# The scan of an RWKV-7 layer: products in 64x64 quarters of TensorE, keys scaled by a diagonal product, and another order within a chunk

## The chip, the cores and the metric

The kernel runs on one core of a Trainium2 chip. Its metric is the device time of one execution in microseconds (us). Several runs give a median; one more execution was recorded by the hardware profiler, and its span and its rows are what the text reads. Engines are named as in the profile: PE (TensorE's matrix products), PEld (its weight loads), DVE (VectorE), ACT (ScalarE), POOL (GpSimd), SP (SyncE, which here issues most DMAs). "L1700" is line 1700 of the kernel's file. PSUM is the memory that PE writes, in banks of 512 float32 columns.

## What is computed

A two-layer decoder trunk on 1024 positions of width 1024, in float32: an RG-LRU block, cross-attention into 256 memory tokens and an MLP in layer 0; RWKV-7 time mixing, cross-attention and an MLP in layer 1. The change lies in the RWKV-7 mixer, whose recurrence per head (16 heads of 64) is, cut from the reference:

```python
def step(state, inp):
    r_t, w_t, k_t, v_t, a_t, b_t = inp
    sa = jnp.einsum('bhij,bhj->bhi', state, a_t)
    state = (state * w_t[:, :, None, :] + sa[..., None] * b_t[:, :, None, :]
             + v_t[..., None] * k_t[:, :, None, :])
    y_t = jnp.einsum('bhij,bhj->bhi', state, r_t)
    return state, y_t
```

Then y is normalised per head, scaled, shifted, given a bonus term and a gate, and multiplied by w_o.

## The kernel before, in words

Projections, decays, Gram matrices and triangular inverses of all positions are made ahead, and parked in DRAM: a and r rows (MVd), b and k rows (STd), inverses (XTd), values (Vd), gates (G1d, G2d). The scan then walks through 16 chunks of 64 positions. Eight feature tiles q of 128 partitions hold two heads each: head half h is the partition half `hr[h]`. A chunk's heads are worked on in two groups, m (or g) = 0 and 1, of four tiles each.

For each chunk c a tile `sv` holds, per head, the state in the partition half `hr[h]` and the chunk's values in the other. The steps, with their lines in the kernel before:

- `scan_scale` (L1689, POOL): multiplies b and k by the decay at the chunk's end (`pcc`). Two instructions of 128x512.
- `scan_gram` (L1700, PE): products of b and k with a and r, 128 x 128 per head, in two PSUM banks, one for each h. `scan_mask` (L1710, DVE): times a triangular mask, into `gw`. L1712 (ACT): a itself is copied over one corner of `gw`, after the mask.
- `scan_keys` (L1724, PE; L1725, ACT): transposes the scaled b and k into `gk`.
- `values` (L1811, PE; L1813, ACT): W = `gw` times `sv`, copied out of PSUM. It needs the state, and both mask and corner of `gw`.
- `decayed` (L1818, POOL): the state times the decay, into `pcs`.
- `from_state` (L1823, PE): r times the state, the first part of the output Y.
- `solved` (L1829, PE; L1831, DVE): the inverse times W, scaled by `db` (1/d), written over the state's half of `sv`.
- `update` (L1836, PE; L1838, DVE): `gk` times `sv`, plus `pcs`: the state of chunk c + 1.
- `output` (L1843, PE; L1845, ACT): the rest of Y, and its copy out.
- `post_var` (L1736, ACT: eight squarings with sums; L1738 and L1739, POOL), `post_norm` (L1744, DVE), `flip_out` (L1751, PE transposes; L1756, DVE; L1757, POOL): normalisation, turning and gating of chunks c - 1 and c - 2.

Gram, mask and keys are those of chunk c + 1, made a chunk ahead. The order within a chunk is a list, `todo`, written out by hand; a wrapper pins what it calls to that order on each engine. So each engine works its steps off as a queue: an instruction that waits holds all behind it. Other work (the splitting of w_o into two parts, L233 and L234) is put between by a scheduler, which also orders SP's queue, except where it is pinned.

Loads are made for two chunks at a time: L1645 (b and k), L1648 (a and r, four buffers that are filled far ahead), L1659 (inverses), L1672 (values), L1676 (gates). They come from a pool of 45 buffers "u"; a load is issued when a buffer is free. Two PSUM pools of four banks serve the scan. Most matmul loops run over h inside q, so neighbouring products use different halves of PE's rows or columns; the tile position follows from the operands' partitions. One earlier step, the Gram matrices of the preparation (L1418), already gives 64x64 tile positions in all four quarters in turn:

```python
for par, h in ((0, 0), (1, 1), (1, 0), (0, 1)):
    sc = slice((2 * c + par) * 64, (2 * c + par) * 64 + 64)
    mm(pg[h][hr[par], c * 64:c * 64 + 64], a[hr[h], sc], at[hr[h], sc], start=True, stop=True, tile_position=(h * 64, par * 64))
```

Of the kernel before, what the change touches and what calls it, by code (L numbers as in the profile page):

```python
# [1281 lines left out]
def rwkv(self, X, xt, lw_wa, lw_g, post, mid):  # L1282
# [214 lines left out]
        xts[f] = XT  # L1497

    def merge_store(f):
        MQ(nc, f).dma_start(XTd[:, f, :], xts.pop(f))  # L1500

    def aside(step):

# [67 lines left out]
    def evac_v(f, p):  # L1571
        cs = slice(f * 128, f * 128 + 128)
        vt = self.unit()
        nc.scalar.copy(vt, p)
        if f == 1:

            self.depth, self.ahead = DA
            with self.behind():
                self.advance(self.taken - 1)
        pr, kp = ld.pop(f)  # L1580
        nc.vector.scalar_tensor_tensor(pr, pr, self.col("r_k", f), kp, ALU.mult, ALU.mult)
        prs = self.split(pr)


        if f % 2 == 0:
            vk[:] = [self.unit() for _ in range(2)]
        for e in range(2):
            pt = self.bank()
            for i in range(4):
                tt = e * 4 + i  # L1590
                mm(pt[:, i * 128:i * 128 + 128], vt[:, tt * 128:tt * 128 + 128], self.center, start=True, stop=True)
            nc.scalar.copy(vk[e].rearrange("p (t h g i) -> p t h g i", h=2, g=2, i=64)[:, :, :, f % 2, :],
                           pt.rearrange("p (t h i) -> p t h i", h=2, i=64))
            if f % 2 and e == 0:

                for d in range(2):
                    for h in range(2):
                        nc.sync.dma_start(sv0[d][hr[1 - h], h * 512 + (f - 1) * 64:h * 512 + (f + 1) * 64],
                                          vk[0].rearrange("p (t h i) -> p t h i", h=2, i=128)[hr[d], 0, h, :])
            if f % 2:  # L1600
                for h in range(2):
                    nc.sync.dma_start(Vd[e * 512:e * 512 + 512, h, (f - 1) * 64:(f + 1) * 64].rearrange("(t p) i -> p t i", p=128),
                                      vk[e].rearrange("p (t h i) -> p t h i", h=2, i=128)[:, :, h, :])
        g1 = self.unit()
        for e in range(2):
            s = slice(e * 512, e * 512 + 512)
            bp = self.bank()
            for i in range(2):
                mm(bp, self.ones_r, prs[i][:, s], start=i == 0, stop=i == 1)
            nc.vector.tensor_mul(vt[:, s], vt[:, s], bp)  # L1610
            gp = self.bank()
            self.mm3(gp, (g2[0][:, cs], g2[1][:, cs]), (hg[0][:, s], hg[1][:, s]), True, True)
            nc.scalar.activation(g1[:, s], gp, AF.Copy, scale=self.col("gn_g", f))
            nc.vector.scalar_tensor_tensor(vt[:, s], vt[:, s], self.col("gn_b", f), gp, ALU.add, ALU.mult)
        for src, dst in ((g1, G1d), (vt, G2d)):
            for h in range(2):
                nc.sync.dma_start(dst[(f % 2) * 64:(f % 2) * 64 + 64, (f // 2) * 2 + h, :], src[h * 64:h * 64 + 64, :])

    def early(f):
        cs = slice(f * 128, f * 128 + 128)  # L1620
# [10 lines left out]
    def load(n):  # L1631
# [7 lines left out]
        mv = mvb[n % 4]  # L1639
        sts = []  # L1640
        for g in range(2):
            st = self.unit().rearrange("p (e q w t) -> p e q w t", e=2, q=4, w=2)
            for e in range(2):
                es = slice(n * 128 + e * 64, n * 128 + e * 64 + 64)
                nc.sync.dma_start(st[:, e], STd[:, 4 * g:4 * g + 4, :, es])  # L1645
            sts.append(st)
        for w in range(2):
            nc.sync.dma_start(mv[:, :, w, :], MVd[:, :, w, ts])  # L1648
        pcs = self.unit().rearrange("p (e q t) -> p e q t", e=2, q=8)
        for e in range(2):  # L1650
            c, cs = 2 * n + e, slice(e * 64, e * 64 + 64)
            cst[c] = dict(st=[t[:, e] for t in sts], mv=mv[:, :, :, cs],
                          pcs=pcs[:, e], pcc=self.pc[:, c * 8:c * 8 + 8].unsqueeze(2), gw=[])

    def load_solved(n):
# [7 lines left out]
    def load_late(n):  # L1663
# [13 lines left out]
        for e in range(2):  # L1677
            cst[2 * n + e].update(sv=svs[e], gs=gs)

    def scan_scale(c):  # L1680

        if c >= 15:
            return
        s = cst[c]
        s["sc"] = self.unit()
        scv = s["sc"].rearrange("p (q w t) -> p q w t", q=8, w=2)
        for g in range(2):
            qs = slice(4 * g, 4 * g + 4)
            nc.gpsimd.tensor_tensor(scv[:, qs], s["st"][g], s["pcc"][:, qs].unsqueeze(3).broadcast_to([128, 4, 2, 64]), ALU.mult)  # L1689

    def scan_gram(c, g):

# [2 lines left out]
        s = cst[c]  # L1695
        s["pv", g] = [self.bank(h).rearrange("p (q w) -> p q w", q=4) for h in range(2)]
        for q in range(4):
            for h in range(2):
                with self.line("gram"):
                    mm(s["pv", g][h][:, q, :], s["st"][g][hr[h], q].rearrange("p w t -> p (w t)"), s["mv"][hr[h], 4 * g + q],  # L1700
                       start=True, stop=True)

    def scan_mask(c, g):
        if c >= 16:
# [7 lines left out]
            nc.scalar.copy(gw[hr[h], :, h, 0:64], s["mv"][hr[h], 4 * g:4 * g + 4, 0, :])  # L1712
        s["gw"].append(gw)

    def scan_keys(c, g):

        if c >= 15:
            return
        s = cst[c]
        if not g:  # L1720
            s["gk"] = self.unit().rearrange("p (q h i) -> p q h i", q=8, h=2)
        tp = self.bank(g).rearrange("p (q h i) -> p q h i", q=4, h=2)
        for q in range(4):
            nc.tensor.transpose(tp[:, q].rearrange("p h i -> p (h i)"), s["sc"][:, (4 * g + q) * 128:(4 * g + q) * 128 + 128], self.ident)  # L1724
        nc.scalar.copy(s["gk"][:, 4 * g:4 * g + 4], tp)  # L1725
# [52 lines left out]
    for c in range(2):  # L1778
        scan_scale(c)
        for g in range(2):  # L1780
            scan_gram(c, g)
            scan_mask(c, g)
            scan_keys(c, g)
    load_late(0)
    self.psum_layout("banks")
    for h in range(2):
        nc.gpsimd.memset(cst[0]["sv"][hr[h], :, h, :], 0.0)
    for c in range(16):
        if c == 15:
            self.psum_layout("mixed")  # L1790
# [4 lines left out]
                    load_solved(c // 2 + 1)  # L1795
                load_late(c // 2 + 1)
        s = cst[c]
        sv, mv, pcc, xtc, pcs = s["sv"], s["mv"], s["pcc"], s["xt"], s["pcs"]
        dbv = self.db[:, 0:128].rearrange("p (q a t) -> p q a t", a=2, t=8)[:, :, c % 2, c // 2:c // 2 + 1]
        W, U, S, wsb = [], [], [], []  # L1800
        y = self.unit()
        yp = self.bank(c)
        Y = yp.rearrange("p (q i) -> p q i", i=64)

        def values(m):

# [1 line left out]
            reg = [ph[:, x * 256:x * 256 + 256].rearrange("p (q i) -> p q i", i=64) for x in range(2)]  # L1808
            W.append(reg[0]); U.append(reg[1]); S.append(reg[0])
            for q, h in heads:  # L1810
                mm(W[m][hr[h], q, :], s["gw"][m][:, q, h, 0:64], sv[:, m * 4 + q, h, :], start=True, stop=True)  # L1811
            w_ = y[:, 512 + m * 256:768 + m * 256].rearrange("p (q i) -> p q i", i=64)
            nc.scalar.copy(w_, W[m])  # L1813
            wsb.append(w_)

        def decayed(m):
            for h in range(2):
                nc.gpsimd.tensor_tensor(pcs[hr[h], m * 4:m * 4 + 4, :], sv[hr[h], m * 4:m * 4 + 4, h, :],  # L1818
                                        pcc[hr[h], m * 4:m * 4 + 4].broadcast_to([64, 4, 64]), ALU.mult)

        def from_state(m):
            for q, h in heads:
                mm(Y[hr[h], m * 4 + q, :], mv[hr[h], m * 4 + q, 1, :], sv[hr[h], m * 4 + q, h, :],  # L1823
                   start=(m == 0 and q == 0), stop=False)

        def solved(m):
            qs = slice(m * 4, m * 4 + 4)
            for q, h in heads:
                mm(U[m][hr[h], q, :], xtc[hr[h], m * 4 + q, :], wsb[m][hr[h], q, :], start=True, stop=True)  # L1829
            for h in range(2):  # L1830
                nc.vector.tensor_tensor(sv[hr[h], qs, h, :], U[m][hr[h]], dbv[hr[h], qs].broadcast_to([64, 4, 64]), ALU.mult)  # L1831

        def update(m):
            qs = slice(m * 4, m * 4 + 4)
# [5 lines left out]
        def output():  # L1840
            for m in range(2):
                for q, h in heads:
                    mm(Y[hr[h], m * 4 + q, :], s["gw"][m][:, q, h, 64:128], sv[:, m * 4 + q, h, :], start=False,  # L1843
                       stop=(m == 1 and q == 3))
            nc.scalar.copy(y[:, 0:512], yp)  # L1845
# [34 lines left out]
    w = I["b_w_o"][0]  # L1880
    rows = []
    for q in range(4):
        for h in range(2):
# [51 lines left out]
```

## Time and profile before

| | us |
|---|---|
| median of 3 runs | 2841.48 |
| lowest and highest | 2838.39, 2846.89 |
| profiled execution | 2839.18 |
| its span | 2837.5 |
| PE busy, whole span | 2765.8 (97%) |
| DVE, ACT, POOL busy | 1867.1, 1422.8, 907.3 |
| scan, first values burst to last output | about 1741 to 1893 |

The profiled execution took 1.7 us more than its span, which runs from its first to its last recorded instruction. A timeline row gives a start in us from the span's start, the time covered, the engine, the line, the operation, output and input names, partitions x elements, and how many instructions were merged; in brackets, what the engine waited for. For matmuls "64*128" are the rows and columns of the array in use. A float32 product is two PE instructions, a transpose one. "Granted clock" is the share of TensorE's full clock that the throttle let through. A row of a group of instructions ends with busy time, mean duration in ns, and the idle time ahead of them.

### The profile page before, as it was taken

What the parts mean: (1) busy time and instruction counts of PE and PEld (TensorE: products, weight loads), DVE (VectorE), ACT (ScalarE), POOL (GpSimd) and SP (SyncE); (2) the same over time, 40 slices, a digit from 0 to 9 for tenths busy, and PEclk for the clock granted to TensorE, in tenths of its full rate; (3) what the DMA queues carried; (4) which work ended last, traced back from release to release, by engine and by line L of the source; (5) the groups of instructions that cost most, each with busy time, mean ns of one, the idle gap of its engine ahead of it and who ended that gap; (6) DMA issues with size and microseconds to landing.
All of it is one profiled execution on the core that took longest, in us unless ns stands there. A gap on an engine that the chain in (4) does not pass through costs nothing.

```text
span 2837.5 us, 42691 instructions
## 1 busy us (share of the span) xinstructions
PE 2765.8 (97%) x16955; PEld 2310.6 (81%) x16955; DVE 1867.1 (66%) x2017; ACT 1422.8 (50%) x2194; POOL 907.3 (32%) x962
## 2 busy tenths in 40 slices
PE   7999999999999999999999999999999999999998
PEld 6888788888888888887777777888888888888887
DVE  5477557658454577898685834785675755467778
ACT  6456355545545553346672534664563644555333
POOL 2000113014666510013088223853203376640002
PEclk9999999999999999999999999999999999999999
DMA  8212352323454554423558799962222355474453
GB/s 266 75 45 75 104 171 79 103 84 104 148 164 153 206 205 156 155 98 126 170 146 228 218 247 244 238 158 96 79 93 89 99 167 162 141 244 168 149 177 120
DMA packets 383912, 421.92 MB, mean 149 GB/s; under 512 B 91504, under 2 KB 294496, under 8 KB 383712
## 3 DMA queue, kind: packets, MB, share of 16 engines
q1 hardware_dynamic: 371680, 379.19, 44.1%
q0 software_dynamic: 11568, 39.41, 3.8%
q8 instruction: 133, 2.18, 0.3%
q14 instruction: 67, 0.55, 0.1%
q10 hardware_dynamic: 464, 0.59, 0.1%
HBM read 283.79 MB, written 134.74 MB: 148 GB/s over the span
## 4 chain that ended last, share of the span: by engine, by line
PE 44%; DVE 4%; ACT 2%; DMA 2%; issue 1%; SPq 1%; POOL 1%; DVEq 0%; POOLq 0%; ACTq 0%
PE q L318 8%; PE q L319 8%; PE q L320 8%; PE p L318 4%; PE p L320 4%; PE p L319 4%; PE q L1700 1%; DVE u L234 1%; DMA u<-d 1%; PE q L1811 1%; PE q L1823 1%; PE q L1348 1%; PE q L1724 1%; DMA u<-in_b_w_rkv 1%; PE q L1836 0%
## 5 line engine op out<-in xcount | busy, mean ns | idle before, releaser
L234 DVE TENSOR_TENSOR u<-u,u 128x1024 fp32r<-128x1024 f32 (+1 forms) x602 | 813.0, 1381 | 346.4 <-ACT u L233 331.1
L233 ACT CAST u<-u 128x1024 fp32r<-128x1024 f32 (+1 forms) x602 | 591.8, 1020 | 446.6 <-DVE u L1077 224.6
L318 PE MATMUL q<-u,u 128*128 128x512 f32 (+1 forms) x1952 | 744.7, 383 | 4.4 <-DVE u L370 2.1
L319 PE MATMUL q<-u,u 128*128 128x512 f32 (+1 forms) x1952 | 745.0, 382 | 0.0
L320 PE MATMUL q<-u,u 128*128 128x512 f32 (+1 forms) x1952 | 739.7, 382 | 0.0
L318 PE MATMUL p<-u,u 128*128 128x512 f32 (+1 forms) x1472 | 553.5, 378 | 14.5 <-ACT u L233 6.4
L319 PE MATMUL p<-u,u 128*128 128x512 f32 (+1 forms) x1472 | 552.5, 375 | 3.7 <-DVE u L234 3.5
L320 PE MATMUL p<-u,u 128*128 128x512 f32 (+1 forms) x1472 | 551.2, 375 | 4.0 <-DVE u L234 3.9
L328 POOL TENSOR_SCALAR s<-s 128x1 f32<-128x1 f32 x97 | 43.7, 451 | 1252.0 <-ACT u L326 1250.1
L318 PEld LDWEIGHTS q<-u,u 128*128 128x128 f32 x1952 | 366.9, 188 | 77.3 <-ACT u L361 1.5
L320 PEld LDWEIGHTS q<-u,u 128*128 128x128 f32 x1952 | 366.8, 188 | 71.2
L319 PEld LDWEIGHTS q<-u,u 128*128 128x128 f32 x1952 | 367.0, 188 | 70.1
L318 PEld LDWEIGHTS p<-u,u 128*128 128x128 f32 x1472 | 279.7, 190 | 67.1 <-issue 8.6
L320 PEld LDWEIGHTS p<-u,u 128*128 128x128 f32 x1472 | 279.9, 190 | 55.2 <-DVE u L234 6.2
L319 PEld LDWEIGHTS p<-u,u 128*128 128x128 f32 x1472 | 280.1, 190 | 54.4 <-DVE u L234 6.7
L443 POOL TENSOR_TENSOR u<-u,u 128x512 f32<-128x512 f32 x120 | 188.1, 1573 | 6.2 <-PE q L319 2.6
L1135 DVE TENSOR_TENSOR z<-z,q 128x512 f32<-128x512 f32 x192 | 130.7, 683 | 80.2 <-PE q L320 80.2
L320 PE MATMUL q<-z,u 128*128 128x512 f32 x320 | 124.5, 389 | 2.1 <-DVE u L234 2.1
L318 PE MATMUL q<-z,u 128*128 128x512 f32 x320 | 124.8, 390 | 0.0
L319 PE MATMUL q<-z,u 128*128 128x512 f32 x320 | 124.5, 389 | 0.0
L444 POOL TENSOR_TENSOR u<-u 128x512 f32<-128x512 f32 x40 | 68.2, 1704 | 146.2 <-DVE u L234 102.9
L1032 POOL TENSOR_TENSOR u<-u,u 128x512 f32<-128x512 f32 x32 | 46.1, 1441 | 181.7 <-ACT u L1021 172.6
(253 smaller groups left out, 3321.5 us busy)
## 6 DMA issues: line engine op xcount, KB each, us to landing
u<-d SPq DMA_DIRECT2D x194, 512.0 KB, 4.8
d<-u SPq DMA_DIRECT2D x109, 512.0 KB, 3.0
d<-u POOLq DMA_DIRECT2D x68, 512.0 KB, 3.7
d<-u SPq DMA_DIRECT2D x132, 256.0 KB, 3.4
u<-in_m_w_up SPq DMA_DIRECT2D x64, 512.0 KB, 5.4
u<-in_m_w_down SPq DMA_DIRECT2D x64, 512.0 KB, 7.3
u<-in_c_w_kv SPq DMA_DIRECT2D x32, 512.0 KB, 6.5
u<-in_b_w_rkv SPq DMA_DIRECT2D x24, 512.0 KB, 7.1
```

The costliest lines, as they stand in the source:

```text
L233: self.nc.scalar.copy(hv, src)
L234: (eng or self.nc.vector).tensor_tensor(lv, src, hv, ALU.subtract)
L318: mm(o, ah, bh, start=first, stop=False, **kw)
L319: mm(o, ah, bl, start=False, stop=False, **kw)
L320: mm(o, al, bh, start=False, stop=last, **kw)
L328: nc.gpsimd.tensor_scalar(v, ss, 1.0 / n, eps, ALU.mult, ALU.add)
L443: sub = lambda o, x, y: nc.gpsimd.tensor_tensor(o, x, y, ALU.subtract)
L444: nc.gpsimd.tensor_tensor(s[:, a], f1[:, a], f1[:, b], ALU.add)
L1032: tt(s1, r21, r22, ALU.add)
L1135: nc.vector.tensor_add(to_, to_, o)
L1348: mm(p, wa2[i][r, cs], hwa[j][r, s], start=n == 0, stop=n == 2)
L1700: mm(s["pv", g][h][:, q, :], s["st"][g][hr[h], q].rearrange("p w t -> p (w t)"), s["mv"][hr[h], 4 * g + q], start=True, stop=True)
```

## The change

It touches the scan, and what is stored for it.

- `scan_gram` makes four 64x64 products per head pair instead of two of 64x128. `scan_keys` no longer transposes: b and k in quarters are multiplied by a diagonal matrix of the decays, which `scan_scale` makes from an identity `id64` in one POOL instruction of 128x512. The keys' PSUM is split by h instead of by group.
- `values`, `from_state`, `output` and `solved` write W, U and Y of head half h and group m to the partition half h xor m. So `from_state` and `solved` can run over the four pairs of `quads`, each in another quarter. Y gets two banks, one for each m, and two copies. The inverses and gates of tiles 4 to 7, and the rows of w_o, are stored or loaded with their halves swapped to fit.
- b and k are loaded with both chunks of a pair in one DMA: runs of 128 elements instead of 64, four DMAs of 256 KB become two of 512 KB. The inverses are stored in two DMAs of 64 partitions instead of one of 128.
- `decayed` of chunk c + 1 and `scan_scale` of c + 2 follow the update of chunk c.
- `todo` has another order.

```diff
     def scan_gram(c, g):
...
-            for h in range(2):
+            for h, w in quads:
                 with self.line("gram"):
-                    mm(s["pv", g][h][:, q, :], s["st"][g][hr[h], q].rearrange("p w t -> p (w t)"), s["mv"][hr[h], 4 * g + q],
-                       start=True, stop=True)
+                    mm(s["pv", g][h][hr[w], q, :], s["st"][g][hr[h], q, w, :], s["mv"][hr[h], 4 * g + q],
+                       start=True, stop=True, tile_position=(h * 64, w * 64))
...
+    quads = [(0, 0), (1, 1), (0, 1), (1, 0)]
...
-        for g in range(2):
-            qs = slice(4 * g, 4 * g + 4)
-            nc.gpsimd.tensor_tensor(scv[:, qs], s["st"][g], s["pcc"][:, qs].unsqueeze(3).broadcast_to([128, 4, 2, 64]), ALU.mult)
+        s["sc"] = self.unit()[:, 0:512].rearrange("p (q i) -> p q i", i=64)
+        nc.gpsimd.tensor_tensor(s["sc"], self.id64.unsqueeze(1).broadcast_to([128, 8, 64]),
+                                s["pcc"].broadcast_to([128, 8, 64]), ALU.mult)
...
+        for q in range(8):
+            for h, w in quads:
+                mm(tps[h][hr[w], q, :], s["st"][q // 4][hr[h], q % 4, w, :], s["sc"][hr[h], q, :],
+                   start=True, stop=True, tile_position=(h * 64, w * 64))
+        for h in range(2):
+            nc.scalar.copy(s["gk"][:, :, h, :], tps[h])
...
+        def from_state():
+            Y.extend(self.bank(m)[:, 0:256].rearrange("p (q i) -> p q i", i=64) for m in range(2))
+            for q in range(4):
+                for h, m in quads:
+                    mm(Y[m][hr[h ^ m], q, :], mv[hr[h], m * 4 + q, 1, :], sv[hr[h], m * 4 + q, h, :],
+                       start=q == 0, stop=False, tile_position=(h * 64, (h ^ m) * 64))
+
+        def solved():
+            for q in range(4):
+                for h, m in quads:
+                    r = h ^ m
+                    mm(U[m][hr[h], q, :], xtc[hr[r], m * 4 + q, :], wsb[m][hr[r], q, :], start=True, stop=True,
+                       tile_position=(r * 64, h * 64))
...
-        todo = [(decayed, 0), (decayed, 1)] if c < 15 else []
-        if c:
-            todo += [(scan_scale, c + 1)]
-        todo += [(values, 0), (from_state, 0), (values, 1), (from_state, 1)]
+        more = c and c < 15
+        todo = [(values, 0), (values, 1), (from_state,)]
         if c:
             todo += [(post_var, c - 1)]
-        todo += [(solved, 0), (solved, 1)]
+        if more:
+            todo += [(scan_gram, c + 1, 0), (scan_mask, c + 1, 0)]
+        todo += [(solved,)]
+        if more:
+            todo += [(scan_keys, c + 1), (scan_gram, c + 1, 1)]
+        if c < 15:
+            todo += [(update, 0), (update, 1), (decayed, c + 1), (scan_scale, c + 2)]
+        todo += [(output,)]
+        if more:
+            todo += [(scan_mask, c + 1, 1)]
         if c > 1:
             todo += [(flip_out, c - 2)]
-        if c:
-            todo += [(scan_gram, c + 1, 0)]
-        if c < 15:
-            todo += [(update, 0), (update, 1)]
-        if c:
-            todo += [(scan_keys, c + 1, 0), (scan_keys, c + 1, 1), (scan_mask, c + 1, 0), (scan_gram, c + 1, 1), (scan_mask, c + 1, 1)]
-        todo += [(output,)]
         if c:
             todo += [(post_norm, c - 1)]
```

How the instructions then stand: on DVE, one chunk late in the scan, before. L1831 multiplies by 1/d, L1756 gates a turned chunk, L1838 adds the state, L1710 masks, L1744 normalises; "q" is a PSUM bank, "u" a buffer.

```order
L1831 TENSOR_TENSOR u_16112<-q_16646,db 64x256 x2
L1831 TENSOR_TENSOR u_16112<-q_16664,db 64x256 x2
L1756 TENSOR_TENSOR u_16553<-q_16713,u_15762 128x8x64
L1838 TENSOR_TENSOR u_16462<-u_16106,q_16646 64x256 x2
L1838 TENSOR_TENSOR u_16462<-u_16106,q_16664 64x256 x2
L1710 TENSOR_TENSOR u_16763<-q_16720,mask 128x4x128
L1710 TENSOR_TENSOR u_16763<-q_16721,mask 128x4x128
L1710 TENSOR_TENSOR u_16778<-q_16768,mask 128x4x128
L1710 TENSOR_TENSOR u_16778<-q_16769,mask 128x4x128
L1744 TENSOR_TENSOR u_16472<-u_16472,g_16682 128x512
```

And now, a chunk at the same place; L1843 is the multiplication, L1850 the addition, L1768 the gating, L1756 the normalisation.

```order
L1756 TENSOR_TENSOR u_16568<-u_16568,g_16813 128x512
L1710 TENSOR_TENSOR u_17069<-q_17051,mask 128x4x128
L1710 TENSOR_TENSOR u_17069<-q_17052,mask 128x4x128
L1843 TENSOR_TENSOR u_16558<-q_17012,db 64x256
L1843 TENSOR_TENSOR u_16558<-q_17002,db 64x256 x2
L1843 TENSOR_TENSOR u_16558<-q_17012,db 64x256
L1850 TENSOR_TENSOR u_16561<-u_16555,q_17002 64x256 x2
L1850 TENSOR_TENSOR u_16561<-u_16555,q_17012 64x256 x2
L1710 TENSOR_TENSOR u_17193<-q_17131,mask 128x4x128
L1710 TENSOR_TENSOR u_17193<-q_17132,mask 128x4x128
L1768 TENSOR_TENSOR u_17203<-q_17198,u_16131 128x8x64
```

The first two masks moved from behind the additions to ahead of the multiplications; the last two stay behind the additions.

On SP, ahead of chunk 2, before: "z" are the buffers of a and r, L1676 loads gates, L1672 values.

```order
L1648 DMA z_14688<-d_10180 128x8x128 x4
L1676 DMA u_14412<-d_10177 128x8x128
L1676 DMA u_14413<-d_10178 128x8x128
L1672 DMA u_14422<-d_10175 64x512 x2
L1672 DMA u_14425<-d_10175 64x512 x2
```

And now:

```order
L1648 DMA z_14819<-d_10180 128x8x128 x4
L1648 DMA z_13731<-d_10180 128x8x128
L1676 DMA u_14494<-d_10177 128x8x128
L1676 DMA u_14495<-d_10178 128x8x128
L1672 DMA u_14508<-d_10175 64x512 x2
L1672 DMA u_14511<-d_10175 64x512 x2
```

A fifth load of a and r, for a later pair of chunks, moved ahead of the values of chunks 2 and 3.

More of the change, by code (lines that the diff above doesn't have):

```diff
@@ L1641, in load @@
         for g in range(2):
[L1642 to L1645, printed above, removed]
+            st = self.unit().rearrange("p (q w t) -> p q w t", q=4, w=2)
+            nc.sync.dma_start(st, STd[:, 4 * g:4 * g + 4, :, ts])
             sts.append(st)
@@ L1651, in load @@
             c, cs = 2 * n + e, slice(e * 64, e * 64 + 64)
[L1652 removed]
+            cst[c] = dict(st=[t[:, :, :, cs] for t in sts], mv=mv[:, :, :, cs],
                           pcs=pcs[:, e], pcc=self.pc[:, c * 8:c * 8 + 8].unsqueeze(2), gw=[])
@@ L1787, in rwkv @@
         nc.gpsimd.memset(cst[0]["sv"][hr[h], :, h, :], 0.0)
+    decayed(0)
     for c in range(16):
@@ L1814, in values @@
             wsb.append(w_)
[L1816 to L1831, printed above, removed]
+        def from_state():
[10 more added lines that the diff above has]
+                       tile_position=(r * 64, h * 64))
+            for m in range(2):
+                qs = slice(m * 4, m * 4 + 4)
+                for h in range(2):
+                    nc.vector.tensor_tensor(sv[hr[h], qs, h, :], U[m][hr[h]], dbv[hr[h], qs].broadcast_to([64, 4, 64]), ALU.mult)
         def update(m):
@@ L1882, in rwkv @@
     for q in range(4):
-        for h in range(2):
+        for h in (0, 1) if q < 2 else (1, 0):
             rows.append([w[(2 * q + pp) * 128 + h * 64:(2 * q + pp) * 128 + h * 64 + 64, :] for pp in range(2)])
```

42 lines of the change are left out of this document (22 added, 20 removed).

## The prediction

> **What bounds the kernel now.** I read the busy time by stretches first, then the timeline of one chunk engine by engine, then the waits and SP's queue. The change touches only the scan of the RWKV-7 layer, some 150 of 2837.5 us. Busy time in it (us, PE, PEld, DVE, ACT, POOL, granted clock, DMA share, GB/s):
>
> ```profile
> 1740.00:1760.00 20.00, 16.33 (x383) 14.44 (x381) 11.73 (x23) 9.02 (x33) 11.24 (x14) 1.00 0.95 259
> 1760.00:1770.00 10.00, 10.00 (x189) 8.94 (x186) 5.38 (x12) 4.25 (x22) 4.74 (x6) 0.83 1.12 253
> 1770.00:1870.00 100.00, 99.21 (x2150) 88.77 (x2146) 74.71 (x144) 62.18 (x263) 81.95 (x94) 1.00 1.04 239
> ```
>
> From 1770 on PE is full. One chunk on PE (start, time covered, line, shape, instructions; a float32 product is two instructions):
>
> ```profile
> 1798.27 1.15 PE L1843 MATMUL q<-u,u 128*64 128x64 f32 x32
> ...
> 1800.43 0.69 PE L1811 MATMUL q<-u,u 128*64 128x64 f32 x16
> 1801.05 0.68 PE L1823 MATMUL q<-u,z 64*64 64x64 f32 x16
> 1801.56 1.10 PE L1829 MATMUL q<-u,u 64*64 64x64 f32 x32
> 1802.60 0.66 PE L1751 MATMUL q<-ident,u 128*128 128x128 f32 x4
> 1803.18 1.16 PE L1700 MATMUL q<-z,u 64*128 64x128 f32 x16
> 1804.27 1.15 PE L1836 MATMUL q<-u,u 128*64 128x64 f32 x32
> 1805.35 1.09 PE L1724 MATMUL q<-ident,u 128*128 128x128 f32 x8
> 1806.38 1.16 PE L1700 MATMUL q<-z,u 64*128 64x128 f32 x16
> 1807.47 0.74 PE L1843 MATMUL q<-u,u 128*64 128x64 f32 x18
> ```
>
> From output to output this chunk takes 9.20 us with no pause. An instruction of 64 columns lasts 218 ns (group row below), so 32 of them in 1.10 us follow one another every (1.10 - 0.22)/31 = 28.5 ns; 16 are 0.455 us. Yet values (L1811) to from_state (L1823) is 0.62: where the tile shape changes, 0.16 us go by. Nine such places cost 1.4 us a chunk. The average chunk, between the second values bursts of chunks 2 and 14, takes (1877.78 - 1761.36)/12 = 9.70 us:
>
> ```profile
> 1759.36 1.02 PE L1811 MATMUL q<-u,u 128*64 128x64 f32 x16 [2.79 <-DMA u<-d]
> 1760.31 1.12 PE L1823 MATMUL q<-u,z 64*64 64x64 f32 x16
> 1761.36 1.12 PE L1811 MATMUL q<-u,u 128*64 128x64 f32 x16
> ...
> 1877.78 0.93 PE L1811 MATMUL q<-u,u 128*64 128x64 f32 x16
> ...
> 1892.89 0.50 PE L318 MATMUL p<-u,u 128*128 128x512 f32 x1
> ```
>
> **The change on PE.** Its form of product runs already, in the Gram matrices of the preparation (L1418: 64x64, all four quarters in turn):
>
> ```profile
> 1376.42 1.16 PE L1418 MATMUL q<-u,u 64*64 64x64 f32 x64
> 1377.51 0.73 PE L1348 MATMUL q<-u,u 64*128 64x512 f32 x4
> ```
>
> That is (1.16 - 0.22)/63 = 15.0 ns each, half of 28.5. So per chunk: from_state and solved, 32 instructions each, fall from 0.91 to 0.48 (estimate 32 x 15.0). The keys become 64 of them, 0.96, against eight transposes that also start 1.09 before what follows. The two Gram bursts had both row halves at work on 128 columns in 1.09 - 0.16 = 0.93 each; cut into quarters they are twice as many instructions, each half as wide, and I leave 0.93. Values, update, output and flip stay: 0.91, 0.91, 0.91, 0.47. Work: 0.48 + 0.48 + 0.96 + 1.86 + 2.73 + 0.47 = 6.98. The shape now changes four times (values to from_state, Gram to update, output to flip, flip to values): 0.64. PE falls to 7.6 us a chunk. If PE still set the pace, that were 2.1 x 12 = 25 us.
>
> **The change in the order.** I think PE no longer sets it. The groups of the stretch 1770 to 1866, ten chunks (busy, mean ns), and starts on DVE and ACT:
>
> ```profile
> L1710 DVE TENSOR_TENSOR u<-q,mask 128x512 f32<-128x512 f32 x40 | 25.0, 684 | 0.3
> L1831 DVE TENSOR_TENSOR u<-q,db 64x256 f32<-64x256 f32 x40 | 16.9, 423 | 19.7 <-PE q L1829 18.7
> L1744 DVE TENSOR_TENSOR u<-u,g 128x512 f32<-128x512 f32 x10 | 8.3, 826 | 0.0
> L1829 PE MATMUL q<-u,u 64*64 64x64 f32 x320 | 11.4, 218 | 0.1
> L1689 POOL TENSOR_TENSOR u<-u,pc 128x512 f32<-128x512 f32 x20 | 24.0, 1221 | 0.8
> L1736 ACT ACTIVATE u<-u 128x64 f32<-128x64 f32 x80 | 19.3, 242 | 0.2
> ```
> ```profile
> 1797.10 2.49 DVE L1710 TENSOR_TENSOR u<-q,mask 128x512 f32<-128x512 f32 x4
> 1802.34 1.78 DVE L1831 TENSOR_TENSOR u<-q,db 64x256 f32<-64x256 f32 x4 [2.04 <-PE q L1829]
> 1804.16 0.69 DVE L1756 TENSOR_TENSOR u<-q,u 128x512 f32<-128x512 f32 x1
> 1805.00 1.77 DVE L1838 TENSOR_TENSOR u<-u,q 64x256 f32<-64x256 f32 x4 [0.15 <-PE q L1836]
> ```
> ```profile
> 1796.35 1.07 ACT L1725 COPY u<-q 128x512 f32<-128x512 f32 x2 [2.46 <-PE q L1724]
> ...
> 1799.62 0.40 ACT L1712 COPY u<-z 64x256 f32<-64x256 f32 x1 [0.19 <-DVE u L1710]
> ...
> 1801.17 0.37 ACT L1813 COPY u<-q 128x256 f32<-128x256 f32 x1 [0.26 <-PE q L1811]
> ```
> ```profile
> 1737.26 0.99 PE L1700 MATMUL q<-z,u 64*128 64x128 f32 x12
> ```
> ```profile
> 1738.45 0.69 DVE L1710 TENSOR_TENSOR u<-q,mask 128x512 f32<-128x512 f32 x1 [0.59 <-PE q L1700]
> ```
>
> The new order closes a loop through five engines' queues, each in order. On DVE the first two masks now stand ahead of the four multiplications by 1/d, and wait for a Gram burst that PE gives after from_state; the last two masks stand behind the four state additions; ACT copies behind them; and the second values burst of the next chunk needs those copies. From one second values burst (0) to the next:
> - from_state starts at 0.62, Gram at 0.62 + 0.48 = 1.10, the first mask 1.19 later (1737.26 to 1738.45): 2.29.
> - Masks start every (2.49 - 0.68)/3 = 0.60, so the second ends at 2.29 + 0.60 + 0.68 = 3.57. The multiplications start at 3.49, every (1.78 - 0.42)/3 = 0.45; the three that the update's first half needs are done at 4.82.
> - ACT is later: mask copy 0.40 to 4.02 (0.04 to start), two key copies 1.07 to 5.09 (the eight squarings, 19.3/10 = 1.9 us, end at 3.1 ahead of them). The update starts at 5.13.
> - First addition 0.73 later (1804.27 to 1805.00): 5.86. Four at 0.45: 7.66.
> - Two masks: 0.60 + 0.68, to 8.95. Copy 0.04 + 0.40 and PE's start 0.04: 9.43 us.
>
> In this loop PE works but for 2.8 us; what it saves outside it turns into pauses, some 1.3 us before the second values burst and 0.5 before the update. DVE has 4 x 0.60 + 8 x 0.45 + 0.69 + 0.83 = 7.5 us of work a chunk, POOL saves one of its two scalings (1.22), both under 9.43. Gain: (9.70 - 9.43) x 12 = 3.2 us.
>
> A rule of the Trainium skill speaks against solved: TensorE: Matmul & The Clock Gate, Part 3 (What overlaps and what doesn't), lets a weight load overlap running products only in another row group, and the new order of solved takes one row half twice running. Values already take all 128 rows each time, and keep 28.5 ns by alternating column halves, so the trace does not bear it out. By the rule solved would be 0.91 instead of 0.48, the keys and their copies 0.18 later, and the sum 12 x 0.18 = 2.2 us worse.
>
> **Head.** Chunk 2 waits for its values from DRAM (2.79 us, above). SP's queue sets that:
>
> ```profile
> 1740.52 7.63 SPq L1648 DMA_DIRECT2D z<-d  x4
> 1748.20 3.25 SPq L1676 DMA_DIRECT2D u<-d  x2
> 1751.49 4.26 SPq L1672 DMA_DIRECT2D u<-d  x4
> ```
>
> In the new order a fifth L1648 load goes ahead of L1672: 7.63/4 = 1.9 us. Chunk 2 starts at 1761.3; its second values burst follows directly, 0.95 later, so at 1762.2 against 1761.36: 0.85 lost. The clock of 0.83 there makes bursts some 1.7 times as long (1.05 for 0.62); the new first loop has about 0.9 more of such work in its path. What chunks 0 and 1 save is lost in that same wait; so are the two diagonal scalings, decayed(0) and the keys as products ahead of them. If the cover is gone, it is 2 us gained.
>
> **Tail.** From 1877.78 to 1892.89 are 15.11 us. New: 9.43, then second values, copy and start 1.15, solved 0.48 + 0.28, multiplications 1.78, output 1.09: 14.2. Gain 0.9.
>
> **Other edits.** Key loads in 512 KB instead of two of 256 KB: in steady state SP waits for buffers that compute frees, and no engine of the chunk waits for a transfer, so nothing; if the pace were DMA's, up to a quarter of the packet time of the keys. The solved inverses stored in halves, the gate stores and the rows of w_o in another order: same bytes, beside PE's full work; between -1 and +1.
>
> Sum: 3.2 - 0.85 - 0.9 + 0.9 = 2.4 us less than the profiled 2839.18. The median of the runs is 2841.48, 2.3 above that; so 2839. A measurement of this kernel can tell about 0.3%, 8.5 us.
>
> **Rivals.**
> 1. The loop is looser, and PE's 7.6 or DVE's 7.5 binds. For it: 99.21 of 100 us busy on PE is what binds now. Against: the order of DVE and ACT, where nothing can pass. Then (9.70 - 7.7) x 12 = 24, less head, plus tail: 2818.
> 2. Quarters that write one PSUM bank from both row halves do not run four wide. L1418 gives each row half a bank of its own; the new from_state and solved do not. For it, a rule of the Trainium skill: TensorEngine Tiling (Array Packing), Gotcha 1, says different row tiles cannot access one bank at a time. Against it: the old from_state (L1823) writes both halves to one bank at the same 28.5 ns as values. Bounds are 15.0 and 28.5; I take 15.0, since from_state's four quarters differ from L1418's only in the bank. At 28.5 the loop is 9.43 + 0.43 + 0.18 = 10.04, slower than 9.70: (10.04 - 9.70) x 12 + 0.85 + 0.9 - 0.5 = 5.3 slower, 2847. It decides from about 19 ns on.
> 3. No quarter product here runs four wide, Gram's 128 columns and the keys included. Then PE alone holds the update until 0.62 + 0.91 + 1.86 + 0.91 + 1.82 + 1.86 = 7.98 instead of 5.13: 12.3 a chunk, (12.3 - 9.70) x 12 = 31 us slower, 2873. Against: L1418 does run so.
>
> **How the numbers follow.** Forecast 0.63, rival 1 0.16, rival 2 0.14, rival 3 0.07. A loop of 9 steps read to some 0.05 us each is good to 0.4 us a chunk, 5 us; the forecast alone is 2833 to 2845. The range takes in rival 2 above and part of the way to rival 1 below: 2829 to 2848. Faster by over 0.3%: rival 1 and 0.09 of the forecast, 0.25. Slower: rival 3, a third of rival 2, 0.02 of the forecast: 0.13. Within: 0.62.
>
> **What would show it.** Right: L1829's successor at half its start distance; PE pausing before the second values burst for ACT's mask copy and before the update for ACT's key copy; DVE waiting for the Gram burst at its first mask; chunks of 9.4 us; chunk 2 starting near 1761 by a wait on DMA. Wrong: no pause on PE in chunks under 9, or from_state over 0.7 us.

## The result, and the profile after

The changed kernel takes 2866.59 us (median of 6 runs, 2860.18 to 2872.14) against 2839.67 for the kernel before on the same chip: 1.0093 times as long, 95% interval 1.008 to 1.0107. It is 0.9% slower where 2839 was forecast, above the range of 2829 to 2848. The profiled execution took 2860.18 us, 21.0 more than that of before; it is the shortest of the six, so the trace shows 21.0 of the medians' 26.9.

The new lines: Gram L1700, masks L1710, corner copies L1712, keys L1724 (PE) and L1727 (ACT), scale L1688, values L1822 and their copy L1824, from_state L1831, solved L1838 and 1/d L1843, update L1848 and addition L1850, output L1855, turning L1763, decayed L1737.

Busy time by stretches after (us, PE, PEld, DVE, ACT, POOL, granted clock, DMA share, GB/s):

```profile
1740.00:1760.00 20.00, 14.54 (x452) 13.29 (x456) 9.65 (x21) 8.08 (x33) 9.15 (x12) 0.91 1.04 273
1760.00:1770.00 10.00, 5.51 (x201) 5.12 (x193) 3.44 (x8) 3.67 (x20) 2.02 (x3) 0.89 1.07 264
1770.00:1870.00 100.00, 77.10 (x2452) 68.30 (x2452) 62.83 (x119) 51.69 (x217) 60.18 (x70) 0.94 0.86 216
1870.00:1910.00 40.00, 33.42 (x1127) 29.28 (x1122) 30.36 (x58) 25.35 (x108) 24.26 (x27) 1.00 0.36 96
```

PE was busy for 99.21 us of the 100 from 1770 on before. Now it is busy for 77.10, and every other engine for less: nothing that computes is full. The trace's records give the second values burst of chunk 2 at 1758.39 and of chunk 14 at 1898.32, so (1898.32 - 1758.39)/12 = 11.66 us a chunk, against 9.70. One chunk on PE:

```profile
1785.43 0.69 PE L1831 MATMUL q<-u,z 64*64 64x64 f32 x32
1785.95 1.05 PE L1700 MATMUL q<-z,u 64*64 64x128 f32 x32
1786.83 0.64 PE L1838 MATMUL q<-u,u 64*64 64x64 f32 x32
1787.29 0.53 PE L1724 MATMUL q<-u,u 64*64 64x64 f32 x22
1790.02 0.85 PE L1724 MATMUL q<-u,u 64*64 64x64 f32 x41 [2.21 <-issue]
...
1791.74 1.15 PE L1848 MATMUL q<-u,u 128*64 128x64 f32 x32
1792.72 1.34 PE L1855 MATMUL q<-u,u 128*64 128x64 f32 x32
1793.99 0.66 PE L1763 MATMUL q<-ident,u 128*128 128x128 f32 x4
1794.57 0.69 PE L1822 MATMUL q<-u,u 128*64 128x64 f32 x16
1795.45 0.33 PE L1822 MATMUL q<-u,u 128*64 128x64 f32 x2 [0.20 <-ACT u L1712]
```

The products do what they were meant to: from_state takes (0.69 - 0.22)/31 = 15.2 ns an instruction, solved (0.64 - 0.22)/31 = 13.5. But PE stops for 2.21 us in the middle of the keys, after 22 of their 64 instructions, where the next one needs nothing new. PE's waits in the scan (line, releaser, total us, times, longest):

```profile
PE q L1724 <- issue: 15.3, 7, 3.3
PE q L1700 <- issue: 7.3, 5, 2.7
PE q L1848 <- issue: 5.5, 3, 2.8
PE q L1822 <- ACT u L1712: 4.8, 15, 0.4
PE q L1838 <- issue: 1.7, 1, 1.7
```

"issue" is time in which the engine waited for nothing that the profile shows. It hits seven different lines, often inside a burst. Of the 21.0 us, the twelve chunks lost 12 x 1.96 = 23.5; chunk 2 came 3.0 earlier (the preparation had ended 3 earlier); the rest is +0.5.

**Where PE stops.** I counted PE's records (weight loads, products, its semaphore waits) from the start of the trace, and set each long pause beside the packets of the DMA queue q8, of kind "instruction". An extract:

```
PE's record  pause from .. to    us     q8 packet from .. to    end of packet to PE's next
20161        1747.43 .. 1750.95  3.53   1748.36 .. 1749.57      1.39
20417        1755.45 .. 1756.34  0.90   1753.55 .. 1755.03      1.32
20673        1760.77 .. 1762.68  1.92   1760.00 .. 1761.15      1.54
20929        1765.12 .. 1768.17  3.06   1765.36 .. 1766.50      1.67
21441        1776.31 .. 1778.65  2.34   1776.05 .. 1777.15      1.50
21697        1784.27 .. 1785.00  0.73   1782.27 .. 1783.43      1.57
21953        1787.60 .. 1790.02  2.42   1787.18 .. 1788.59      1.43
```

The profile marks 21 waits of PE between 1738 and 1910 with "issue". All 21 fall on a record whose number leaves 193 when divided by 256, and in each PE goes on 1.3 to 1.7 us after a q8 packet has landed. Kernel before and after, q8 in the page's table of DMA queues (packets, MB, share):

```profile
q8 instruction: 133, 2.18, 0.3%
```
```profile
q8 instruction: 144, 2.36, 0.4%
```

2.36 MB in 144 packets are 16.4 KB each. PE's records are 36,832, close to 144 x 256 = 36,864; before, they are 34,167, close to 133 x 256 = 34,048. Counted by place it comes out exactly: the records 193 (counted from 0), 449, 705 and so on, each 256 further, are 144 after and 133 before, as many as the packets, and so it is in the trace of every experiment below (133 to 144 of each). So q8 brings PE its own program, 256 instructions a packet, and a block of 256 starts at each of these records. During the first pause of the table (the stretch in which that packet runs) PE does nothing while DVE works on:

```profile
1748.36:1749.57 1.21, 0.00 (x0) 0.00 (x0) 1.20 (x5) 0.40 (x1) 1.15 (x1) 1.00 1.16 298
```

One packet runs for each block. Among the 17 paused blocks between 1762 and 1885 it starts 2.44 us (mean) after PE has entered the block before, takes 1.25, and PE goes on 1.48 later: 5.2 us from block to block. It looks as if the next block is asked for when the one before it is read, and no earlier. Outside the scan, where a block lasts some 29 us, the packet can start up to 5.3 us, or 43 records, ahead of PE's entry into the block before, as if PE's reading ran that far ahead of its work; in no trace is it more. Before, a chunk was 204 product instructions, each with its weight load: 408 instructions, 1.6 blocks in 9.70 us, 6.1 us a block, and just two pauses over 0.25 us in the scan (0.30 and 0.64). Now it is 292 product instructions, 584 in all, 2.28 blocks: 2.28 x 5.1 = 11.6 us. That is no test yet: 5.13 us is the mean of all 25 blocks between 1762 and 1885, which is the measured chunk read another way. (The records give 414 and 587 a chunk, semaphore waits included.)

That is the theory to test: **PE's supply of instructions sets the pace.** Its rivals: the new **order** with its waits or buffers; the new key **loads**; the new products **themselves**.

### The profile page after: what moved, and what is told of

It is laid out like the page before. It is cut to its first block, busy times and chain, and to the rows that moved or that the text cites. A ratio compares the mean times of both kernels' runs of the same rounds, so it can differ in the third digit from the quotient of the medians.

```text
span 2858.5 us, 45340 instructions
## 1 busy us (share of the span) xinstructions
PE 2753.1 (96%) x18307; PEld 2298.6 (80%) x18307; DVE 1867.1 (65%) x2017; ACT 1426.1 (50%) x2210; POOL 900.2 (31%) x951
## 3 DMA queue, kind: packets, MB, share of 16 engines
q8 instruction: 144, 2.36, 0.4%
## 4 chain that ended last, share of the span: by engine, by line
PE 40%; DVE 5%; issue 3%; ACT 3%; DMA 2%; POOL 1%; SPq 1%; DVEq 0%; POOLq 0%; ACTq 0%
PE q L318 8%; PE q L320 8%; PE q L319 8%; PE p L318 3%; PE p L319 3%; PE p L320 3%; DMA u<-d 1%; PE q L1700 1%; DVE u L234 1%; PE q L1848 1%; PE q L1348 1%; PE q L1724 1%; ACT u L326 1%; ACT u L233 0%; PE q L1822 0%
```

## The experiments

Figures behind each: the median, then the ratio to the kernel before on the same chip with its 95% interval; "chunk" is the mean from chunk 2 to 14 in the profiled execution; "pauses" is the sum of the pauses over 0.2 us at a block's first instruction, in the scan (for the changed kernel, 37.6). Chunk and pauses belong to the profiled execution, whose own time is given where it lies over 2 us from the median.

### Gram and keys as before, in the new order

```diff
-            for h, w in quads:
+            for h in range(2):
...
-                    mm(s["pv", g][h][hr[w], q, :], s["st"][g][hr[h], q, w, :], ... tile_position=(h * 64, w * 64))
+                    mm(s["pv", g][h][:, q, :], s["st"][g][hr[h], q].rearrange("p w t -> p (w t)"), ...)
```

Keys, their scaling and the key loads likewise.

> The changed kernel with its Gram matrices and keys made as before (Gram 128 columns at a time, keys by eight transposes of scaled keys, and the key loads per chunk that these need); the new order and the 64x64 products of from_state and solved stay. PE then has 408 instructions a chunk instead of 584. Instruction supply (PE is given 256 instructions at a time, and asks for the next block only when it enters the one before it, some 5.1 us a block): 408/256 x 5.1 = 8.1 us a chunk is no longer the bound, the pauses at every 256th instruction nearly vanish, chunks fall from 11.66 to the loop of the new order, 9.4 to 9.7; total 2834 to 2842. Order (the new order's waits or its buffers make the pauses): chunks stay near 11.7, total 2858 to 2868.

2839.70 us, 1.0 (0.999 to 1.0009), chunk 9.75, pauses 1.3. PE's largest waits:

```profile
PE q L1823 <- ACT u L1716: 8.8, 26, 0.5
PE q L1823 <- DMA u<-d: 6.2, 1, 6.2
PE q L1849 <- DVE u L1844: 2.1, 2, 1.4
PE q L1856 <- DVE u L1844: 0.9, 1, 0.9
PE q L1832 <- issue: 0.6, 1, 0.6
```

The pauses are gone with the new order and the quartered from_state and solved in place. What is left is the wait that the prediction drew: values (L1823) for the corner copy behind the last mask (L1716).

### Only Gram and keys in quarters, in the kernel before

The same edit the other way round, in the kernel before:

```diff
-            for h in range(2):
+            for h, w in quads:
...
-            todo += [(scan_keys, c + 1, 0), (scan_keys, c + 1, 1), (scan_mask, c + 1, 0), ...]
+            todo += [(scan_keys, c + 1), (scan_mask, c + 1, 0), ...]
```

> The kernel before with nothing changed but the Gram matrices and the keys, which are made from 64x64 products (584 instructions a chunk on PE instead of 408, and less array time for them); order, loads, from_state and solved are those of before. Instruction supply: 584/256 x 5.1 = 11.6 us a chunk, 12 x (11.6 - 9.7) = 23 slower, total 2855 to 2866, with pauses at every 256th instruction of PE. Order: this order has no pauses, so chunks of 9.2 to 9.7, total 2832 to 2842.

2860.45 us, 1.0077 (1.0062 to 1.0092); the profiled execution, 2867.57, is the slowest of the four; chunk 11.87, pauses 31.2. All that are marked "issue" stand at 193 of 256; the largest:

```profile
PE q L1845 <- issue: 7.5, 3, 3.1
PE q L1700 <- issue: 4.9, 2, 2.6
PE q L1724 <- issue: 4.4, 3, 1.6
PE q L1831 <- issue: 3.4, 2, 2.2
```

The old order pauses too, once it has 584 instructions; and these products, all of which run four wide here, make the kernel slower.

### The changed kernel with the old key loads, and with the old order

```diff
-            nc.sync.dma_start(st, STd[:, 4 * g:4 * g + 4, :, ts])
+            for e in range(2):
+                es = slice(n * 128 + e * 64, n * 128 + e * 64 + 64)
+                nc.sync.dma_start(st[:, e], STd[:, 4 * g:4 * g + 4, :, es])
```

> The changed kernel with the key loads of before (four of 256 KB per pair of chunks instead of two of 512 KB); all else as changed. Instruction supply: the same 584 instructions, so 2857 to 2870. Loads (a key load that lands late holds PE in the keys): back to 2836 to 2845.

2864.47 us, 1.0081 (1.0066 to 1.0097); profiled, 2857.88, chunk 11.31, pauses 33.9. Not the loads.

```diff
-        todo = [(values, 0), (values, 1), (from_state,)]
+        todo = [(decayed, c)] if c < 15 else []
+        if c:
+            todo += [(scan_scale, c + 1)]
+        todo += [(values, 0), (values, 1), (from_state,)]
...
+        if c:
+            todo += [(scan_keys, c + 1), (scan_mask, c + 1, 0), (scan_gram, c + 1, 1), (scan_mask, c + 1, 1)]
```

> The changed kernel with its steps put back into the order of before (decayed and scale first, Gram and masks behind solved, keys behind the update); all products, the scaling and the loads as changed: 584 instructions a chunk. Instruction supply: 11 to 12 us a chunk whatever the order, total 2852 to 2867. Order: without the loop of the new order PE's 7.6 us or DVE's 7.5 binds, total 2812 to 2835.

2865.86 us, 1.0088 (1.0073 to 1.0103), chunk 11.82, pauses 34.5. Not the order (from_state and solved stay one step each, where the old order had them by group). Four kernels with 584 instructions and different orders and loads give 11.3 to 11.9 us a chunk.

### A dose: 472 and 520 instructions a chunk

Of the first experiment's edit only the keys, then only Gram (with the key loads):

> The changed kernel with only the keys as before (scaled keys, eight transposes): 472 instructions of PE a chunk instead of 584. Instruction supply, a dose: 472/256 x 5.1 = 9.4 us a chunk, as long as the loop of the new order, so 9.5 to 10.3 with a few pauses left; total 2840 to 2849, between the changed kernel (2866) and the one with Gram whole too (2840). If it is not the count but the keys' products themselves that stall (their bank halves, their stationary operands), all pauses go: 2836 to 2841.

2845.50 us, 1.0024 (1.0015 to 1.0034); profiled, 2848.82, chunk 10.28, pauses 18.9.

> The changed kernel with only the Gram matrices as before (128 columns at a time, and the key loads per chunk that this needs): 520 instructions of PE a chunk. Instruction supply: 520/256 x 5.1 = 10.4 us a chunk, total 2846 to 2855, above the one with whole keys. If the keys' products themselves stall, the pauses stay: 2860 to 2868.

2851.28 us, 1.0041 (1.0028 to 1.0055); profiled, 2848.63, chunk 10.45, pauses 14.2. In one table, with the estimate of 5.1 us a block of 256:

```
instructions a chunk    408       472       520       584
5.1 us x blocks         8.1       9.4      10.4      11.6
chunk measured          9.75     10.28     10.45     11.66
median of the kernel  2839.7    2845.5    2851.3    2866.6
profiled execution    2839.8    2848.8    2848.6    2860.2
```

The medians rise with the count, and no one product carries the pauses: with whole keys they are still there, at other lines. The two in the middle are close, though: their intervals just overlap, and in their profiled executions, of equal length, there was more pause at 472 than at 520. Where the estimate comes near the loop's own time both are exceeded, as they would be if a slow packet is not made up for by a fast one. No run adds instructions without also changing products; what tells the count from the products is the place of the pauses, at a block's first instruction whatever its line.

### Fewer loads beside the scan

```diff
-            nc.sync.dma_start(st, STd[:, 4 * g:4 * g + 4, :, ts])
+            if n < 2:
+                nc.sync.dma_start(st, STd[:, 4 * g:4 * g + 4, :, ts])
+            else:
+                st = mv[:, 4 * g:4 * g + 4]
...
-        for w in range(2):
+        for w in range(2 if n < 4 else 0):
```

and the gates likewise.

> The changed kernel with part of its loads left out: from the third pair of chunks on, the keys and the gates are not loaded but read from the tile of the other operand in their place, and that tile itself isn't loaded again from the fifth pair on (so other numbers are computed, with the same instructions, 584 a chunk on PE). Instruction supply: the request for a block waits behind data packets, 2.2 us of its 5 in the middle of the scan; with under half the data in flight a block takes 3.5 to 4, 584/256 x 3.7 = 8.4 us a chunk, so the loop of the new order binds, 9.4 to 10; total 2834 to 2845. If blocks take 5 us whatever else moves (a fixed latency, or PE's own rate of taking instructions): 11 to 12 us a chunk, total 2858 to 2868.

2846.37 us, 1.003 (1.0017 to 1.0043), chunk 10.20, pauses 22.2, with the same 144 packets. The stretch, for the changed kernel and for this one, is 0.86 and 0.29 of the DMA engines:

```profile
1770.00:1870.00 100.00, 85.74 (x2918) 76.97 (x2919) 72.90 (x139) 60.24 (x259) 69.39 (x80) 0.97 0.29 78
```

From PE's entry into a block to the start of the next packet it is 1.42 us on average instead of 2.15; a block takes 4.48 us instead of 5.13. So 15.4 of the 37.6 us of pauses go with the data traffic, and what falls is the packet's wait to start. The median falls by some 20 us; the clock's rise from 0.94 to 0.97 is in that too, and was not told apart. I had expected 3.5 to 4 us a block and a median up to 2845: the other part, 1.1 us of transfer and 1.4 behind it, hardly changes with the traffic (1.2 and 1.5 in the changed kernel).

### Only from_state and solved in quarters, in the old order

The edit to `todo` of the old order and the first experiment's edit together.

> What is left of the change when the supply of instructions and the new order are both taken out of it: order, Gram, keys and key loads as before, only from_state and solved as 64x64 products in all four quarters (408 instructions of PE a chunk). Instruction supply: 8.1 us a chunk isn't the bound; PE saves 2 x 0.43 us and two changes of shape of the 9.70, so 8.6 to 9.2 us a chunk if PE binds, total 2826 to 2835, faster than both kernels. Rival: DVE's or the order's waits take it, 9.4 to 9.8 us a chunk, total 2836 to 2842.

2848.76 us, 1.0028 (1.0013 to 1.0042), chunk 9.93. Both expectations fail. Some chunks take the 9.0 us that I expected (the steps to chunks 4, 6 and 8: 9.0, 9.1 and 9.2), others up to 11.5. Two rows of the longest step, to chunk 5:

```profile
1783.75 0.41 PE L1838 MATMUL q<-u,u 64*64 64x64 f32 x8
1785.66 0.45 PE L1838 MATMUL q<-u,u 64*64 64x64 f32 x8 [1.50 <-issue]
```

Six blocks between 1762 and 1885 pause, 5.2 us together; their packets start 3.8 us after the block before is entered. At 9.0 us a chunk a block is used up in 9.0/1.6 = 5.6 us, and a slow packet shows at once. That is 5.2 of the 9.3 us between the upper end, 2835, and the profiled execution's 2844.31; chunk 2 waits 6.41 us for its values besides (2.79 in the kernel before). Whether the two add up, and what else lengthens every other chunk, was not worked out.

### Taking the other waits out

In the first experiment chunk 2 waits 6.22 us for its values from DRAM. The next two load those ahead of the gates and of two loads at L1648:

```diff
-        gs = [self.unit().rearrange("p (k t) -> p k t", t=128) for _ in range(2)]
-        for t, d in zip(gs, (G1d, G2d)):
+        for k in {0: [], 1: [0, 1]}.get(n, [n]):
+            gs = [self.unit().rearrange("p (k t) -> p k t", t=128) for _ in range(2)]
...
-            with (ExitStack() if c else self.behind()):
+            with (ExitStack() if c > 2 else self.behind()):
```

> The kernel before with the values of the second pair of chunks loaded ahead of the gates of the first and of two of the four loads at its L1648: they are issued some 7 us earlier. If chunk 2 waits for them as its trace says (2.79 us), that wait goes and nothing takes its place: 2836 to 2838.5 against 2840. If other work of the head holds chunk 2 just behind them: no change.

2838.16 us, 0.9997 (0.9987 to 1.0006). The 2.79 us wait is gone and chunk 2's second values burst comes 3.75 us earlier (1757.61), but chunk 15's only 1.4 (1885.96 against 1887.40): pauses of 4.4 us (1.1 in the kernel before) have taken the place, the longest 2.59, in blocks whose packets started 3.9 us after the entry. So the kernel before already stands close to this bound.

> The changed kernel with Gram and keys whole and the key loads of before (408 instructions of PE a chunk, 2839.7), and the values of the second pair loaded ahead as in the other one. There chunks 0 and 1 end earlier and chunk 2 waits 6.22 us for them. If the new order's gain in the head is lost in that wait, it comes back: 2832 to 2836. If the pauses at PE's instruction blocks grow when the head is tighter, 2837 to 2841.

2839.00 us, 1.0005 (0.9997 to 1.0014): no gain. The number lies in the second range, but not for its reason: the pauses are 0.8 us. The step from chunk 1 to chunk 2 fell from 15.7 to 9.9 us, but in the profiled execution (2842.07) the scan had begun 6.0 us later (1744.10 against 1738.12), with the stores and loads of the preparation that stand ahead of it. Whether these loads caused that is open.

The next cuts the loop that the prediction found: solved directly behind from_state, so that on DVE the multiplications by 1/d come ahead of the first masks. Keys and Gram change places on PE with that, and the second Gram and mask go behind the update.

```diff
-        if more:
-            todo += [(scan_gram, c + 1, 0), (scan_mask, c + 1, 0)]
         todo += [(solved,)]
         if more:
-            todo += [(scan_keys, c + 1), (scan_gram, c + 1, 1)]
+            todo += [(scan_keys, c + 1), (scan_gram, c + 1, 0), (scan_mask, c + 1, 0)]
...
+        if more:
+            todo += [(scan_gram, c + 1, 1), (scan_mask, c + 1, 1)]
         todo += [(output,)]
```

> As the one before, and with the loop of the new order cut: solved directly behind from_state, then keys, Gram and masks, so that the multiplications by 1/d come ahead of the first masks. Then PE's own 9.0 us a chunk (or DVE's 7.5) binds instead of the loop's 9.4 to 10: 12 x 0.5 = 6 less, 2826 to 2832. Instruction supply: at 9.0 us a chunk a block of 256 is used up in 5.6 us, and the slow ones among the requests (6 us and more) show as pauses: 2832 to 2842.

2833.63 us, 0.9984 (0.9976 to 0.9993): faster than both kernels, and 5.4 us faster than the one before. The loop's 9.4 to 10.1 are gone: most steps take 8.8 to 9.4 us. The median lies in the second range, but the pauses are just 2.1 us; what is lost is lost in the step from chunk 3 to 4, which takes 16.7. There the transposes of the keys wait for their scaling:

```profile
1771.74 1.11 PE L1730 MATMUL q<-ident,u 128*128 128x128 f32 x4 [4.00 <-POOL u L1695]
1773.92 1.12 PE L1730 MATMUL q<-ident,u 128*128 128x128 f32 x4 [1.07 <-POOL u L1695]
```

The scaling, on POOL, had itself waited 5.25 us for a DMA, and SP's queue shows why: the key loads of that pair (L1647) stand behind four loads at L1650:

```profile
1750.18 6.43 SPq L1680 DMA_DIRECT2D u<-d  x4
1756.66 7.24 SPq L1650 DMA_DIRECT2D z<-d  x4
1763.95 6.07 SPq L1647 DMA_DIRECT2D u<-d  x4
```

The last one keeps every pair's loads in turn:

```diff
-            with (ExitStack() if c > 2 else self.behind()):
+            with self.behind():
```

> As whole_values_first_masks_late, with no pair's loads issued ahead of their turn (the order that the kernels before and after keep for the first pair's late loads holds for every pair): two loads of 512 KB at L1650 no longer stand ahead of the keys of the third pair, for whose scaling PE waited 4.00 us in one place there. If that wait is set by SP's queue in the head, most of it goes: 2829 to 2832. If the queue only moves it (the transfers share the same DMA time, and a later pair comes late instead), 2832 to 2836.

2834.55 us, 0.9987 (0.9977 to 0.9997): also faster than both, and no better than the one before it. The wait for the scaling is gone (0.8 us in all), and no later load took its place. The steps to chunks 3 to 8 take 8.8 to 9.4 us, 9.0 on average. Then the pauses are back:

```profile
PE q L1858 <- issue: 4.9, 3, 3.3
PE q L1825 <- ACT u L1718: 2.5, 10, 0.5
PE q L1706 <- issue: 2.3, 2, 1.5
PE q L1851 <- DVE u L1846: 1.7, 2, 1.4
```

Nine blocks between 1762 and 1885 pause, 11.4 us together, and the steps to chunks 9 to 12 take 9.8 to 10.6; the longest pause, 3.5 us, comes behind chunk 15's values. With the loop, the values and the keys out of the way, the supply of instructions holds PE up even at 408 a chunk, in this execution; the one before it had 2.1 us of pauses.

## Why the prediction was wrong, point by point

- **The step that failed** is the cost of the new products: "the keys become 64 of them, 0.96", Gram's are "twice as many instructions, each half as wide, and I leave 0.93", "PE falls to 7.6 us a chunk". So the sum had the loop's 9.43 us as the longest thing in a chunk, and the chunk came out at 11.66. The prediction priced instructions by their time in the array alone and counted an instruction as free where its width halved. The array times were right (13.5 to 15.2 ns for quarters; Gram's 32 in 1.05 us). But 176 more instructions a chunk are 0.69 of a block more, 3.5 us at 5.1 us a block, of which the slack of before (6.1 us a block) covered less than half. The first experiment takes just these away (with Gram, keys and their loads), and 26.9 us go with them; the second adds just these to the kernel before, and 20.2 us come.
- **The rivals** all asked how wide the products run or which engine binds. None asked what supplies PE with instructions. Rivals 2 and 3 are refuted: from_state ran at 15.2 ns with both row halves in one bank. Rival 3's price, 2873, is near the result by chance: its mechanism is not in it.
- **The rule** from TensorE: Matmul & The Clock Gate in the Trainium skill, by which solved would take 0.91, does not hold here either: 13.5 ns an instruction, 0.43 us for 32.
- **The loop** was right, where it can be seen: in the first experiment every other chunk takes 9.4 us against 9.43 worked out, with the wait where it was put, and step by step. Counted from the values row that starts at 1791.01 in its trace, the first mask starts 2.43 us later, the update at 5.07, the first addition at 5.80, the last mask ends at 8.89 and the next values start at 9.38; worked out were 2.29, 5.13, 5.86, 8.95 and 9.43. The chunks between take 9.6 to 10.1; in the longer of them PE's queue has the keys between the two halves of solved, which holds back the update:

```profile
1802.71 0.68 PE L1839 MATMUL q<-u,u 64*64 64x64 f32 x16
1803.33 1.09 PE L1728 MATMUL q<-ident,u 128*128 128x128 f32 x8
1804.35 0.68 PE L1839 MATMUL q<-u,u 64*64 64x64 f32 x16
```

  So its gain of 3.2 us was too high by most of it: 9.66 a chunk from chunk 4 to 14, not 9.43.
- **The head**: the wait of chunk 2 for its values was nearly gone after the change (0.2 us), since pauses had already held chunks 0 and 1; without the pauses it is 6.22, and what those chunks save is indeed lost in it, but for some 0.9 us (second values burst at 1760.45, where 1762.2 was worked out and 1761.36 measured before).
- **The key loads** cost nothing that could be told: 2864.5 with the old ones (2857.9 to 2866.3), 2866.6 with the new (2860.2 to 2872.1).
- **The clock**: 0.94 from 1770 to 1870, against 1.00 before, and 1.00 again without the pauses, in the first experiment:

```profile
1770.00:1870.00 100.00, 92.55 (x2110) 80.15 (x2109) 78.04 (x145) 64.17 (x267) 83.15 (x95) 1.00 1.03 236
```

  What the lower clock adds by itself was not measured.

## What to carry to other kernels

Count instructions as well as array time. Where a loop's products are short, so that 256 of PE's instructions (weight loads among them) would be used up in under the 5 to 6 us that a block took here, cutting a product into smaller ones that run side by side bought nothing: a transpose or a wide product in one instruction cost less than its quarters. Pauses marked "issue" inside a burst of one line, at a fixed distance in PE's instruction count and just behind a packet of the instruction queue, are how it looks in a trace.

## What the runs showed of the hardware

- PE's program came in packets of 16.4 KB on q8, one for each 256 instructions, and in the scan no packet started earlier than 0.4 us ahead of PE's entry into the block before (in long blocks elsewhere 5.3 us, or 43 records). In the changed kernel's scan: 2.2 us to the packet's start (up to 7.7 in one experiment), 1.2 us of transfer, and 1.3 to 1.7 until PE went on, where it had paused. The Trainium skill, Runtime: NRT & Kernel Launch, Instruction fetch mechanics, describes blocks of 256 instructions and a fetch of the next while the current one runs, at a cost that is mostly hidden. The blocks agree, and before the change the cost was hidden but for 1.1 us; after it, it was not: 37.6 us of pauses in 174 us of scan.
- Data on the DMA engines slowed the supply of PE's instructions: with the DMA share at 0.29 instead of 0.86, a block took 4.48 us instead of 5.13.
